# Feed-forward products with the high and low halves of the activations side by side

## The chip, the cores and the metric

One core of a Trainium2 chip runs the whole kernel. The metric is the device time of one execution in microseconds (us); lower is better. The engines are TensorE (PE, with its weight loads shown apart as PEld), VectorE (DVE), ScalarE (ACT), GpSimd (POOL) and SyncE (SP), which issues the transfers.

## The reference

The kernel computes two layers of a hybrid encoder on 256 tokens of width 1024, in float32. What matters here are the feed-forward steps, two in each layer, so four in all:

```
def swiglu_ffn(x, g, wi, wo):
    gate, up = jnp.split(rmsnorm(x, g) @ wi, 2, axis=-1)
    return (jax.nn.silu(gate) * up) @ wo
...
for l in range(DEPTH):                                          # 2
    x = x + 0.5 * swiglu_ffn(x, ffn1_norm[l], ffn1_wi[l], ffn1_wo[l])   # wi 1024 x 5632, wo 2816 x 1024
    h = rmsnorm(x, mix_norm[l])
    ...                                                         # four mixers, merged, through w_out, added to x
    x = x + 0.5 * swiglu_ffn(x, ffn2_norm[l], ffn2_wi[l], ffn2_wo[l])
```

## The kernel before

Activations are held transposed: channels on the 128 partitions, the T = 256 tokens along the columns, so x is KT = 8 tiles of 128x256. A weight tile is 128x128 and is the stationary operand; the activations move past it.

Every float32 operand is split into a high part, rounded to the type float32r, and a low part, what is left. A product is then three matmuls, which mm (L205) issues: high weights by high activations (L207), high weights by low activations (L208), low weights by high activations (L209). All three add into the same 128x256 of PSUM.

Weights come by DMA in chunks of up to 2048 columns and are split on the chip by Weights.split in units of 1024 columns, which are eight tiles: ScalarE writes hi (L109), VectorE writes lo (L110). There are four buffers of each, and W.next splits two units ahead of the one in use. The helper split (L211) does the same for activations: ScalarE at L214 (L217 with a scale), VectorE at L215 (L218).

Norm holds what a feed-forward step or the mixer takes as input: add(k) splits x times the gain, without the normalising factor; square sums squares; scale (L341) sums over partitions on TensorE (tile pr), and GpSimd takes the power -1/2 (rt); scale_rows (L353) spreads it over the partitions with four matmuls into pb (L357) and ScalarE copies it to rr (L365). So the feed-forward products start before the factor is known, and it is multiplied in behind them.

ffn (L381) runs over 11 pairs c of columns of the hidden layer. For each c, gates(c) makes two groups of eight weight tiles by three matmuls into one PSUM bank (pg), ups(c) the same into another (pu). scaled (L392) multiplies each by rr on VectorE (L395), silu applies Silu on ScalarE (L403), hidden multiplies both (L407) and splits the result into hh and hl. For c = 0 the factor is not there yet; its silu and hidden come in c = 1, behind scale_rows. Then come eight groups over 22 weight tiles into po, each added to x by VectorE (L434), after which nxt(n) prepares the norm of the next stage, or writes the output.

The mixer makes a normalised copy of x of its own for its later products: full_norm(k) takes x times gain times rr on VectorE (xnt, L511) and splits it (xnh, xnl).

PSUM has eight buffers of one bank (128x512 float32). The pool m4 has 16 buffers of 128x1040, small has two for each name. The order of instructions on each engine is made by the framework's list scheduler from the order of the program; each engine then works its list in order.

Of the kernel before, what the change touches and what calls it, by code (L numbers as in the profile page):

```python
# [9 lines left out]
F32R = mybir.dt.float32r  # L10
AF = mybir.ActivationFunctionType
ALU = mybir.AluOpType
# [5 lines left out]
T = 256  # L18
P = 128
KT = D // P  # L20
DFF = 2816
KF = DFF // P
# [20 lines left out]
O_N1, O_NM, O_N2 = 0, 8, 16  # L43
# [129 lines left out]
def hybrid_encoder(ctx: ExitStack, tc: tile.TileContext, xT, par, rows, ident_d, flat, out, order=None):  # L173
    nc = tc.nc
    A, V, G, TE = nc.scalar, nc.vector, nc.gpsimd, nc.tensor
# [9 lines left out]
    W = Weights(nc, flat, order, raw_pool, hi_pool, lo_pool)  # L185

    def bank(name):
        return ps.tile([P, 512], F32, tag="ps", name=name)

    def m4(name, dt=F32, cols=1024):  # L190
        assert cols <= 1040
        return mp.tile([P, 1040], dt, tag="m4", name=name, bufs=16)[:, :cols]
# [9 lines left out]
    def small(name, shape, bufs=2):  # L202
        return sp.tile(shape, F32, tag="s_" + name, name=name, bufs=bufs)

    def mm(out, lhs, rhs, start, stop):  # L205

        TE.matmul(out, lhs[0], rhs[0], start=start, stop=False)  # L207
        TE.matmul(out, lhs[0], rhs[1], start=False, stop=False)  # L208
        TE.matmul(out, lhs[1], rhs[0], start=False, stop=stop)  # L209

    def split(hi, lo, src, scale=None):  # L211

        if scale is None:
            a = A.copy(hi, src)  # L214
            b = V.tensor_tensor(lo, src, hi.bitcast(F32), op=ALU.subtract)  # L215
        else:
            a = A.activation(hi, src, AF.Copy, scale=scale)  # L217
            b = V.scalar_tensor_tensor(lo, src, scale, hi.bitcast(F32), op0=ALU.mult, op1=ALU.subtract)  # L218
        return a, b
# [9 lines left out]
    gains, x = xg[:, :KT], xg[:, KT:].rearrange("p (k t) -> p k t", t=T)  # L229
# [11 lines left out]
    def col(l, o, n=1):  # L241
        if l == 0 and o + n <= KT:
            return gains[:, o : o + n]
        return prm[:, l * NPAR + o : l * NPAR + o + n]
# [73 lines left out]
    class Norm:  # L318


        def __init__(self, l, gcol):
            self.l, self.gcol, self.first = l, gcol, l == 0 and gcol == O_N1
            self.hi = [m4("xh", F32R).rearrange("p (k t) -> p k t", t=T) for _ in range(2)]
            self.lo = [m4("xl", F32R).rearrange("p (k t) -> p k t", t=T) for _ in range(2)]
            self.acc, self.squared = small("acc", [P, T]), 0
            self.pairs = [(self.hi[k // 4][:, k % 4, :], self.lo[k // 4][:, k % 4, :]) for k in range(KT)]

        def add(self, k):
            return split(*self.pairs[k], x[:, k, :], scale=col(self.l, self.gcol + k))
# [23 lines left out]
        def scale_rows(self):  # L353

            pb = bank("pb")
            for b in range(2):
                TE.matmul(  # L357
                    pb[:, b * P : (b + 1) * P],
                    self.rt[:, b : b + 1].to_broadcast([P, P]),
                    ident,  # L360
                    start=True,
                    stop=True,
                )
            self.rr = small("rr", [P, T])
            A.copy(self.rr, pb[:, :T])  # L365

    def group(dst, name, l, kts, c0, pairs):

        for i, k in enumerate(kts):
            mm(dst, W.next(name, l, k, c0, P), pairs[i], i == 0, i == len(kts) - 1)  # L370

    def groups(dsts, name, l, kts, c0s, pairs, late):

        cut = len(kts) - late
        for part in (range(cut), range(cut, len(kts))):
            for dst, c0 in zip(dsts, c0s):
                for i in part:
                    mm(dst, W.next(name, l, kts[i], c0, P), pairs[i], i == 0, i == len(kts) - 1)


    def ffn(l, wi, wo, nrm, nxt):  # L381
        hs, ts, hh = [], {}, []

        def gates(c, done=0):
            for j in range(done, 2):
                group(ts["g", c][:, j * T : (j + 1) * T], wi, l, range(KT), (2 * c + j) * P, nrm.pairs)

        def ups(c, done=0):
            for j in range(done, 2):
                group(ts["u", c][:, j * T : (j + 1) * T], wi, l, range(KT), DFF + (2 * c + j) * P, nrm.pairs)  # L390

        def scaled(name, c):  # L392
            t = t2k(name)
            rr2 = nrm.rr.unsqueeze(1).to_broadcast([P, 2, T])
            V.tensor_tensor(  # L395
                t.rearrange("p (j t) -> p j t", t=T), ts.pop((name, c)).rearrange("p (j t) -> p j t", t=T), rr2, op=ALU.mult
            )
            return t

        def silu(c):  # L400
            t = scaled("g", c)
            s = ts["s", c] = t2k("s")
            A.activation(s, t, AF.Silu)  # L403

        def hidden(c):
            u = scaled("u", c)
            V.tensor_tensor(u, u, ts.pop(("s", c)), op=ALU.mult)  # L407
            if c % 2 == 0:
                hh.append((m4("hh", F32R), m4("hl", F32R)))
            o = (c % 2) * 512  # L410
            split(*(h[:, o : o + 512] for h in hh[-1]), u)
            for j in range(2):
                hs.append(tuple(h[:, o + j * T : o + (j + 1) * T] for h in hh[-1]))

        for c in range(KF // 2):
            ts["g", c], ts["u", c] = bank("pg"), bank("pu")
            if c == 0:
                groups((ts["g", 0][:, 0:T], ts["u", 0][:, 0:T]), wi, l, range(KT), (0, DFF), nrm.pairs, 2)
                gates(0, 1)
                nrm.scale()  # L420
                ups(0, 1)
                continue
            gates(c)
            if c == 1:
                nrm.scale_rows()
                silu(0)
                hidden(0)
            silu(c)
            ups(c)
            hidden(c)  # L430
        for n in range(KT):
            po = bank("po")[:, :T]
            group(po, wo, l, range(KF), n * P, hs)
            V.scalar_tensor_tensor(x[:, n, :], po, 0.5, x[:, n, :], op0=ALU.mult, op1=ALU.add)  # L434
            nxt(n)


# [36 lines left out]
    def mixer(l, nrm, tabs, nxt):  # L474
# [26 lines left out]
        evac(pl0, lat, 0, hl, True)  # L501
        evac(pl1, lat, hl, hl, True)


        xnh = [m4("xnh", F32R).rearrange("p (k t) -> p k t", t=T) for _ in range(2)]
        xnl = [m4("xnl", F32R).rearrange("p (k t) -> p k t", t=T) for _ in range(2)]
        xn = [(xnh[k // 4][:, k % 4, :], xnl[k // 4][:, k % 4, :]) for k in range(KT)]

        def full_norm(k):
            t = small("xnt", [P, T])  # L510
            V.scalar_tensor_tensor(t, x[:, k, :], col(l, O_NM + k), nrm.rr, op0=ALU.mult, op1=ALU.mult)  # L511
            split(*xn[k], t)

        qkv = [m3("qkv", cols=N_QKV) for _ in range(2)]
        pq0 = tok_group(C_QKV, hq, "w_in", nrm.pairs, range(KT))
        for k in range(4):
            full_norm(k)
        evac(pq0, qkv, 0, hq, True)
        pq1 = tok_group(C_QKV + hq, hq, "w_in", nrm.pairs, range(KT))
        for k in range(4, KT):  # L520
            full_norm(k)
        evac(pq1, qkv, hq, hq, True)


# [614 lines left out]
```

## Time and profile before

| | us |
|---|---|
| median of three runs (1385.9 to 1386.23) | 1386.22 |
| the profiled execution | 1386.98 |
| its span, first to last instruction | 1385.2 |
| TensorE busy in the span | 1367.8 |
| VectorE busy | 939.7 |
| ScalarE busy | 798.0 |

A group of instructions in a profile row has its line in the kernel, its engine, its operation, the tile written and those read by the program's names, and its shapes; L207 is line 207. The time of one matmul in such a row runs from its start to the end of its result, and matmuls overlap, so the step from one start to the next is shorter than that. Durations are of one profiled execution.

### The profile page before, as it was taken

The numbers are of one execution on the slowest core, as the hardware profiler recorded it, in microseconds if no ns is written. First come the engines' busy times: TensorE is split into PE (matmuls) and PEld (weight loads), VectorE is DVE, ScalarE is ACT, GpSimd is POOL, SyncE is SP. The second block draws the span as 40 slices with busy tenths as digits, with TensorE's granted clock in tenths as the row PEclk, the third lists the DMA queues.
The fourth block names the chain that finished last, engine by engine and source line by source line (L and its number), as shares of the span: only waits on it lengthen the run. The fifth ranks groups of instructions, "written<-read, shape, count | busy, mean of one in ns | idle before, by whom it ended". The sixth has DMA issues, their size and how long they took to land. (4 is left out here: it accounts for less than half of the span.)

```text
span 1385.2 us, 26443 instructions
## 1 busy us (share of the span) xinstructions
PE 1367.8 (99%) x11184; PEld 1356.3 (98%) x11184; DVE 939.7 (68%) x1302; ACT 798.0 (58%) x1224; POOL 90.6 (7%) x126
## 2 busy tenths in 40 slices
PE   8999999999999999999999999999999999999999
PEld 7999999999999999999999999999999999999999
DVE  6666557968966766666566665588698666776653
ACT  6444448788657655444444444487885674554442
POOL 3200002300400000000000000030013000000000
PEclk9999999999999999999999999999999999999999
DMA  7555545434543455555555555455345443555552
GB/s 286 183 183 183 185 173 192 169 128 140 190 177 134 143 185 182 184 189 189 185 181 187 189 186 183 151 183 183 119 151 194 164 153 122 201 181 183 186 204 74
DMA packets 35831, 240.81 MB, mean 174 GB/s; under 512 B 3968, under 2 KB 5376, under 8 KB 9472
## 3 DMA queue, kind: packets, MB, share of 16 engines
q1 hardware_dynamic: 35712, 239.12, 49.0%
q8 instruction: 87, 1.43, 0.4%
q14 instruction: 32, 0.26, 0.1%
HBM read 238.06 MB, written 1.05 MB: 173 GB/s over the span
## 5 line engine op out<-in xcount | busy, mean ns | idle before, releaser
L109 ACT CAST hi<-raw 128x1024 fp32r<-128x1024 f32 (+4 forms) x459 | 475.7, 1037 | 496.1 <-PE po L208 117.8
L110 DVE TENSOR_TENSOR lo<-raw,hi 128x1024 fp32r<-128x1024 f32 (+4 forms) x459 | 553.3, 1208 | 294.4 <-ACT hi L109 293.5
L207 PE MATMUL pg<-xh,hi 128*128 128x256 f32 x704 | 199.0, 283 | 5.8 <-ACT hi L109 5.8
L208 PE MATMUL pg<-xl,hi 128*128 128x256 f32 x704 | 199.5, 283 | 0.0
L209 PE MATMUL pg<-xh,lo 128*128 128x256 f32 x704 | 199.3, 283 | 0.0
L209 PE MATMUL pu<-xh,lo 128*128 128x256 f32 x704 | 198.3, 282 | 0.5 <-DVE lo L110 0.5
L208 PE MATMUL pu<-xl,hi 128*128 128x256 f32 x704 | 198.6, 282 | 0.0
L207 PE MATMUL pu<-xh,hi 128*128 128x256 f32 x704 | 198.5, 282 | 0.0
L208 PE MATMUL po<-hl,hi 128*128 128x256 f32 x704 | 197.9, 281 | 0.0
L209 PE MATMUL po<-hh,lo 128*128 128x256 f32 x704 | 197.4, 280 | 0.0
L207 PE MATMUL po<-hh,hi 128*128 128x256 f32 x704 | 197.3, 280 | 0.0
L207 PE MATMUL pgt<-xnh,hi 128*128 128x256 f32 x512 | 145.7, 285 | 0.0
L208 PE MATMUL pgt<-xnl,hi 128*128 128x256 f32 x512 | 144.6, 282 | 0.0
L209 PE MATMUL pgt<-xnh,lo 128*128 128x256 f32 x512 | 144.0, 281 | 0.0
L207 PEld LDWEIGHTS pg<-xh,hi 128*128 128x128 f32 x704 | 133.7, 190 | 6.1 <-ACT hi L109 6.1
L209 PEld LDWEIGHTS pg<-xh,lo 128*128 128x128 f32 x704 | 133.8, 190 | 0.3 <-DVE lo L110 0.2
L208 PEld LDWEIGHTS pg<-xl,hi 128*128 128x128 f32 x704 | 133.8, 190 | 0.0
L209 PEld LDWEIGHTS pu<-xh,lo 128*128 128x128 f32 x704 | 133.1, 189 | 0.7 <-DVE lo L110 0.7
L208 PEld LDWEIGHTS pu<-xl,hi 128*128 128x128 f32 x704 | 133.1, 189 | 0.0
L207 PEld LDWEIGHTS pu<-xh,hi 128*128 128x128 f32 x704 | 133.0, 189 | 0.0
L207 PEld LDWEIGHTS po<-hh,hi 128*128 128x128 f32 x704 | 132.6, 188 | 0.0
L209 PEld LDWEIGHTS po<-hh,lo 128*128 128x128 f32 x704 | 132.5, 188 | 0.0
(298 smaller groups left out, 2869.3 us busy)
## 6 DMA issues: line engine op xcount, KB each, us to landing
raw<-weights SPq DMA_DIRECT2D x205, 1024.0 KB, 4.8
raw<-weights SPq DMA_DIRECT2D x9, 768.0 KB, 4.3
raw<-weights SPq DMA_DIRECT2D x4, 896.0 KB, 4.6
raw<-weights SPq DMA_DIRECT2D x3, 1008.0 KB, 4.7
raw<-weights SPq DMA_DIRECT2D x5, 512.0 KB, 8.2
out<-xg SPq DMA_DIRECT2D x8, 128.0 KB, 2.5
raw<-weights SPq DMA_DIRECT2D x1, 1016.0 KB, 4.7
raw<-weights SPq DMA_DIRECT2D x1, 968.0 KB, 4.7
```

Source lines behind the costliest of these rows:

```text
L109: a = self.nc.scalar.copy(hi[:, :w], src)
L110: b = self.nc.vector.tensor_tensor(lo[:, :w], src, hi[:, :w].bitcast(F32), op=ALU.subtract)
L207: TE.matmul(out, lhs[0], rhs[0], start=start, stop=False)
L208: TE.matmul(out, lhs[0], rhs[1], start=False, stop=False)
L209: TE.matmul(out, lhs[1], rhs[0], start=False, stop=stop)
```

## The change

In the feed-forward products the high and low parts of an activation tile stand side by side in one tile of 512 columns. mm2 issues two matmuls for a weight tile: high weights by both halves into a whole PSUM bank (512 columns), then low weights by the high half into its first 256 columns. The two halves of a bank are added afterwards: joined copies the second half on ScalarE and adds the first on VectorE; for po, two accumulations into x do it. Each of the four groups of a c has a bank of its own. For c = 0 and 1 the products take x times the gain as before, and joined multiplies by rr; from c = 2 on they take a normalised copy of x, which normalised makes in c = 1, behind scale_rows. scale_rows comes after the first of the two gate groups of c = 1, no longer after both. The mixer's full_norm is replaced by the same function.

```diff
--- before.py
+++ after.py
@@ -208,6 +208,23 @@
         TE.matmul(out, lhs[0], rhs[1], start=False, stop=False)
         TE.matmul(out, lhs[1], rhs[0], start=False, stop=stop)
 
+    def mm2(out, lhs, both, start, stop):
+
+
+        TE.matmul(out, lhs[0], both, start=start, stop=False)
+        TE.matmul(out[:, :T], lhs[1], both[:, :T], start=False, stop=stop)
+
+    def pair_tiles(name, n):
+
+        ts = [m4(name, F32R) for _ in range((n + 1) // 2)]
+        boths = [ts[k // 2][:, k % 2 * 512 : k % 2 * 512 + 512] for k in range(n)]
+        return ts, boths, [(a[:, :T], a[:, T:]) for a in boths]
+
+    def parts(t):
+
+        t3 = t.rearrange("p (k w t) -> p k w t", k=2, t=T)
+        return t3[:, :, 0, :], t3[:, :, 1, :]
+
     def split(hi, lo, src, scale=None):
 
         if scale is None:
@@ -320,10 +337,8 @@
 
         def __init__(self, l, gcol):
             self.l, self.gcol, self.first = l, gcol, l == 0 and gcol == O_N1
-            self.hi = [m4("xh", F32R).rearrange("p (k t) -> p k t", t=T) for _ in range(2)]
-            self.lo = [m4("xl", F32R).rearrange("p (k t) -> p k t", t=T) for _ in range(2)]
+            _, self.boths, self.pairs = pair_tiles("xh", KT)
             self.acc, self.squared = small("acc", [P, T]), 0
-            self.pairs = [(self.hi[k // 4][:, k % 4, :], self.lo[k // 4][:, k % 4, :]) for k in range(KT)]
 
         def add(self, k):
             return split(*self.pairs[k], x[:, k, :], scale=col(self.l, self.gcol + k))
@@ -363,11 +378,25 @@
                 )
             self.rr = small("rr", [P, T])
             A.copy(self.rr, pb[:, :T])
+            self.full = None
+
+        def normalised(self, k):
+
+            if self.full is None:
+                self.full = pair_tiles("xn", KT)
+            t = small("xnt", [P, T])
+            V.scalar_tensor_tensor(t, x[:, k, :], col(self.l, self.gcol + k), self.rr, op0=ALU.mult, op1=ALU.mult)
+            split(*self.full[2][k], t)
 
     def group(dst, name, l, kts, c0, pairs):
 
         for i, k in enumerate(kts):
             mm(dst, W.next(name, l, k, c0, P), pairs[i], i == 0, i == len(kts) - 1)
+
+    def wide(dst, name, l, kts, c0, boths):
+
+        for i, k in enumerate(kts):
+            mm2(dst, W.next(name, l, k, c0, P), boths[i], i == 0, i == len(kts) - 1)
 
     def groups(dsts, name, l, kts, c0s, pairs, late):
 
@@ -379,59 +408,74 @@
 
 
     def ffn(l, wi, wo, nrm, nxt):
-        hs, ts, hh = [], {}, []
-
-        def gates(c, done=0):
-            for j in range(done, 2):
-                group(ts["g", c][:, j * T : (j + 1) * T], wi, l, range(KT), (2 * c + j) * P, nrm.pairs)
-
-        def ups(c, done=0):
-            for j in range(done, 2):
-                group(ts["u", c][:, j * T : (j + 1) * T], wi, l, range(KT), DFF + (2 * c + j) * P, nrm.pairs)
-
-        def scaled(name, c):
+        hs, ts = [], {}
+        NEAR = 2
+
+        def tile_of(c, j, name):
+            ts[name, c, j] = bank("p" + name)
+            return ts[name, c, j]
+
+        def column(name, c, j):
+            return (DFF if name == "u" else 0) + (2 * c + j) * P
+
+        def products(name, c, js=(0, 1)):
+            boths = nrm.boths if c < NEAR else nrm.full[1]
+            for j in js:
+                wide(tile_of(c, j, name), wi, l, range(KT), column(name, c, j), boths)
+
+        def joined(name, c):
+
             t = t2k(name)
-            rr2 = nrm.rr.unsqueeze(1).to_broadcast([P, 2, T])
-            V.tensor_tensor(
-                t.rearrange("p (j t) -> p j t", t=T), ts.pop((name, c)).rearrange("p (j t) -> p j t", t=T), rr2, op=ALU.mult
-            )
+            for j in range(2):
+                p, tj = ts.pop((name, c, j)), t[:, j * T : (j + 1) * T]
+                A.copy(tj, p[:, T:])
+                V.tensor_tensor(tj, p[:, :T], tj, op=ALU.add)
+            if c < NEAR:
+                t3 = t.rearrange("p (j t) -> p j t", t=T)
+                V.tensor_tensor(t3, t3, nrm.rr.unsqueeze(1).to_broadcast([P, 2, T]), op=ALU.mult)
             return t
 
         def silu(c):
-            t = scaled("g", c)
+            t = joined("g", c)
             s = ts["s", c] = t2k("s")
             A.activation(s, t, AF.Silu)
 
         def hidden(c):
-            u = scaled("u", c)
+            u = joined("u", c)
             V.tensor_tensor(u, u, ts.pop(("s", c)), op=ALU.mult)
-            if c % 2 == 0:
-                hh.append((m4("hh", F32R), m4("hl", F32R)))
-            o = (c % 2) * 512
-            split(*(h[:, o : o + 512] for h in hh[-1]), u)
-            for j in range(2):
-                hs.append(tuple(h[:, o + j * T : o + (j + 1) * T] for h in hh[-1]))
+            tiles, boths, _ = pair_tiles("hh", 2)
+            split(*parts(tiles[0]), u.rearrange("p (j t) -> p j t", t=T))
+            hs.extend(boths)
 
         for c in range(KF // 2):
-            ts["g", c], ts["u", c] = bank("pg"), bank("pu")
             if c == 0:
-                groups((ts["g", 0][:, 0:T], ts["u", 0][:, 0:T]), wi, l, range(KT), (0, DFF), nrm.pairs, 2)
-                gates(0, 1)
+                firsts = tile_of(0, 0, "g"), tile_of(0, 0, "u")
+                for part in (range(KT - 2), range(KT - 2, KT)):
+                    for dst, c0 in zip(firsts, (0, DFF)):
+                        for k in part:
+                            mm2(dst, W.next(wi, l, k, c0, P), nrm.boths[k], k == 0, k == KT - 1)
+                products("g", 0, (1,))
                 nrm.scale()
-                ups(0, 1)
+                products("u", 0, (1,))
                 continue
-            gates(c)
             if c == 1:
+                products("g", 1, (0,))
                 nrm.scale_rows()
                 silu(0)
                 hidden(0)
+                products("g", 1, (1,))
+                for k in range(KT):
+                    nrm.normalised(k)
+            else:
+                products("g", c)
             silu(c)
-            ups(c)
+            products("u", c)
             hidden(c)
         for n in range(KT):
-            po = bank("po")[:, :T]
-            group(po, wo, l, range(KF), n * P, hs)
-            V.scalar_tensor_tensor(x[:, n, :], po, 0.5, x[:, n, :], op0=ALU.mult, op1=ALU.add)
+            po = bank("po")
+            wide(po, wo, l, range(KF), n * P, hs)
+            for h in range(2):
+                V.scalar_tensor_tensor(x[:, n, :], po[:, h * T : (h + 1) * T], 0.5, x[:, n, :], op0=ALU.mult, op1=ALU.add)
             nxt(n)
 
 
@@ -501,24 +545,15 @@
         evac(pl0, lat, 0, hl, True)
         evac(pl1, lat, hl, hl, True)
 
-
-        xnh = [m4("xnh", F32R).rearrange("p (k t) -> p k t", t=T) for _ in range(2)]
-        xnl = [m4("xnl", F32R).rearrange("p (k t) -> p k t", t=T) for _ in range(2)]
-        xn = [(xnh[k // 4][:, k % 4, :], xnl[k // 4][:, k % 4, :]) for k in range(KT)]
-
-        def full_norm(k):
-            t = small("xnt", [P, T])
-            V.scalar_tensor_tensor(t, x[:, k, :], col(l, O_NM + k), nrm.rr, op0=ALU.mult, op1=ALU.mult)
-            split(*xn[k], t)
-
         qkv = [m3("qkv", cols=N_QKV) for _ in range(2)]
         pq0 = tok_group(C_QKV, hq, "w_in", nrm.pairs, range(KT))
         for k in range(4):
-            full_norm(k)
+            nrm.normalised(k)
+        xn = nrm.full[2]
         evac(pq0, qkv, 0, hq, True)
         pq1 = tok_group(C_QKV + hq, hq, "w_in", nrm.pairs, range(KT))
         for k in range(4, KT):
-            full_norm(k)
+            nrm.normalised(k)
         evac(pq1, qkv, hq, hq, True)
 
 
```

## Rows read from the trace of the kernel before

**Rows 1.** The page, busy time of each engine, share of the span, instructions.

```profile
PE 1367.8 (99%) x11184; PEld 1356.3 (98%) x11184; DVE 939.7 (68%) x1302; ACT 798.0 (58%) x1224; POOL 90.6 (7%) x126
```

**Rows 2.** Groups by line and form: count | busy us, mean ns of one | idle before, releasers.

```profile
L110 DVE TENSOR_TENSOR lo<-raw,hi 128x1024 fp32r<-128x1024 f32 x422 | 516.8, 1227 | 269.8 <-ACT hi L109 268.8
...
L207 PE MATMUL pg<-xh,hi 128*128 128x256 f32 x704 | 199.0, 283 | 5.8 <-ACT hi L109 5.8
...
L207 PE MATMUL pu<-xh,hi 128*128 128x256 f32 x704 | 198.5, 282 | 0.0
...
L207 PE MATMUL po<-hh,hi 128*128 128x256 f32 x704 | 197.3, 280 | 0.0
...
L395 DVE TENSOR_TENSOR g<-pg,rr 128x512 f32<-128x512 f32 x44 | 30.3, 689 | 14.6 <-PE pg L209 14.5
...
L434 DVE SCALAR_TENSOR_TENSOR xg<-po,xg 128x256 f32<-128x256 f32 x32 | 13.5, 422 | 23.9 <-PE po L209 23.9
...
L961 ACT COPY o<-pov 64x256 f32<-64x256 f32 x32 | 11.8, 368 | 6.0 <-PE pov L959 5.3
...
L511 DVE SCALAR_TENSOR_TENSOR xnt<-xg,prm,rr 128x256 f32<-128x256 f32 x16 | 7.1, 482 | 0.4 <-ACT rr L365 0.4
...
L1013 DVE TENSOR_TENSOR xg<-pw,xg 128x256 f32<-128x256 f32 x16 | 6.8, 422 | 5.1 <-PE pw L209 4.9
```

**Rows 3.** Stretches: c = 2 to 10, then po, of both feed-forward steps of layer 0.

```profile
core 0: us, PE busy (x) PEld busy (x) DVE busy (x) ACT busy (x) POOL busy (x), PEclk, DMA share, GB/s
33.15:136.11 102.96, 102.96 (x866) 102.96 (x865) 66.00 (x77) 48.25 (x55) 10.30 (x32) 1.00 0.54 183
136.11:198.64 62.53, 62.53 (x530) 62.53 (x529) 36.04 (x45) 28.70 (x38) 0.00 (x0) 1.00 0.51 179
...
530.50:632.74 102.24, 102.24 (x866) 102.24 (x865) 67.71 (x73) 48.22 (x54) 0.00 (x0) 1.00 0.53 186
632.74:695.34 62.60, 62.60 (x531) 62.60 (x530) 36.16 (x45) 28.90 (x37) 0.00 (x0) 1.00 0.53 185
```

**Rows 4.** Timeline of PE: first matmuls of ups and of the next ups, 96 steps apart.

```profile
61.75 0.28 PE L207 MATMUL pu<-xh,hi 128*128 128x256 f32 x1
...
73.19 0.28 PE L207 MATMUL pu<-xh,hi 128*128 128x256 f32 x1
```

**Rows 5.** Waits: who waited for whom, us in total, times, longest.

```profile
ACT hi L109 <- PE po L208: 117.8, 72, 2.1
ACT hi L109 <- PE pu L208: 108.9, 73, 2.3
```

**Rows 6.** Timeline of PE in the mixer: 512-column matmuls, twelve from the first row to the last.

```profile
346.42 0.39 PE L207 MATMUL pa<-hi,kvh 128*128 128x512 f32 x1
...
346.88 0.40 PE L209 MATMUL pa<-hi,kvl 128*128 128x512 f32 x1
347.12 0.39 PE L207 MATMUL pa<-hi,kvh 128*128 128x512 f32 x1
347.34 0.39 PE L208 MATMUL pa<-lo,kvh 128*128 128x512 f32 x1
...
349.19 0.27 PE L468 MATMUL pT<-ident,pe 128*128 128x128 f32 x1
```

**Rows 7.** Timeline of PE, second feed-forward step: gates of c = 1, pb, gates of c = 2.

```profile
518.69 0.28 PE L207 MATMUL pg<-xh,hi 128*128 128x256 f32 x1
...
524.37 0.60 PE L357 MATMUL pb<-ident,rt 128*128 128x128 f32 x4
...
530.50 0.28 PE L207 MATMUL pg<-xh,hi 128*128 128x256 f32 x1
```

**Rows 8.** Timeline of ACT in the same place: start us, us.

```profile
525.41 0.36 ACT L365 COPY rr<-pb 128x256 f32<-128x256 f32 x1
```

**Rows 9.** Timeline of DVE right behind it.

```profile
526.68 0.68 DVE L395 TENSOR_TENSOR g<-pg,rr 128x512 f32<-128x512 f32 x1
527.28 0.68 DVE L395 TENSOR_TENSOR u<-pu,rr 128x512 f32<-128x512 f32 x1
```

**Rows 10.** A stretch of the first mixer that holds its normalised copy of x.

```profile
214.25:232.00 17.75, 17.75 (x106) 17.75 (x105) 15.27 (x31) 15.77 (x38) 3.79 (x13) 1.00 0.63 215
```

## Prediction

> **What bounds the kernel now.** I read the page's busy times first, then the groups by line and form, then the stretches of a feed-forward stage, then single steps of TensorE in the timeline. The reader should see in [rows 1] that TensorE is busy for 99% of the span, so that only time on its own queue counts, unless a change leaves it without operands. In [rows 2] the feed-forward products (outputs pg, pu, po) are nine groups of 704 matmuls, of which three are shown: 704 x 3 = 2112 weight tiles, each passed over three times with 256 columns, and hardly any idle time stands before them. The groups' durations of about 282 ns are no prices, since matmuls overlap; the price is the step from one start to the next. [rows 3] gives it by stage: columns of c = 2 to 10 take 102.96 and 102.24 us for 9 x 32 = 288 tiles, 357.5 and 355.0 ns a tile, and the products into po 62.53 and 62.60 us for 176 tiles, 355.3 and 355.7. I take 356 ns a tile, 118.7 ns a matmul; the single stretch in [rows 4] (96 steps from 61.75 to 73.19 us) gives 119.2. In all of these stretches the granted clock is 1.00 and TensorE is never idle. VectorE and ScalarE are busy for 64% and 47% of the first stretch of [rows 3], and the waits in [rows 5] say that the cast of weights waits for TensorE to give a buffer back: weights are ready ahead of time. So 2112 x 0.356 = 752 us of the time are steps of these matmuls and nothing else.
>
> **The matmuls.** Columns per tile stay 768: 3 x 256 before, 512 + 256 after. What goes is one matmul and one weight load of three. If a step is strictly in proportion to columns, nothing is gained. The trace of before has 512-column matmuls in the mixer, with the same 128x128 weight load before each: twelve steps from 346.42 to 349.19 us in [rows 6] are 2.77 us, 231 ns each. Twice 118.7 is 237, so a part of about 6 ns of each step does not grow with its columns. The pair would take 231 + 119 = 349.5 ns against 356: 6.5 ns x 2112 = **-13.7 us**. This is the value I take, because shape, type and load are those of the new matmul. Single steps in [rows 6] go from 220 ns (347.12 to 347.34) to 240 (346.88 to 347.12), with 10 ns of rounding in each; as ends for a mean I take 224 and 236. At 236 a tile saves 1.3 ns, 3 us in all; at 224 it saves 13 ns, 28 us. The trace does not show 512 and 256 columns in turn; I see no reason in it for a different price of the mixed order.
>
> The Trainium skill (TensorE: Matmul & The Clock Gate, Back-to-back issue gap) gives a warm step as columns / 2.4 GHz plus about 2.5 ns; by it the pair would save just that one 2.5 ns, an estimate of 5.3 us, and the sum below would end about 8 us higher. The rows do not agree with it in size: by it 256 columns would take 109 ns, and they take 119.
>
> **Joining the two halves.** Each group of eight tiles now fills a bank of its own (high half and low half of the activations), and per column pair c there are four ScalarE copies of 128x256 from PSUM and four VectorE additions of 128x256. In [rows 2] the nearest rows are the copy of po's kind in the mixer (o<-pov, 368 ns, 64 partitions) and xg<-pw,xg, 422 ns. For c of 2 or more the two scalings by rr (689 ns each) go. VectorE: +4 x 0.42 - 2 x 0.69 = +0.3 us per c; ScalarE: +4 x 0.37 = +1.5 us per c. A c takes TensorE 11.2 us, VectorE now uses 66.00 / 9 = 7.3 and ScalarE 48.25 / 9 = 5.4 of it [rows 3]; 7.6 and 6.9 after. Both lie beside TensorE: nothing. The cover is the weights held ahead; without it the four copies would cost 1.5 us a c. A c holds four of the eight banks; a bank is wanted again after eight groups of 2.8 us and is given back about a microsecond after its group ends: nothing, unless a join is queued behind something late. After the last c, the hidden tile's chain (two copies, two additions, one product, one split, about 3 us) has 20 tiles x 0.35 = 7 us before po wants it: nothing.
>
> **The normalised copy of x.** From c = 2 on, the products take x already normalised: per FFN eight times one VectorE product (482 ns, xnt), one ScalarE cast and one VectorE subtraction (nearest: 422 ns). They can't begin before rr, and c = 2 can't begin without their first result. This is the one new wait, and what queues behind it is TensorE itself. In the second FFN [rows 7] the sums of pb start at 524.37 us after both pg groups of c = 1; rr is written by ScalarE at 525.41 + 0.36, [rows 8]; c = 2 starts at 530.50. The change calls scale_rows after one of the two pg groups, half of 524.37 - 518.69 earlier, so rr comes at about 522.9 and c = 2 wants tile 0 some 7.6 us later and tile 7 after 7 x 0.35 = 2.5 us more: a cover of 10.1 us. In it VectorE has: two scalings, one product and one split for c = 0 (4 x 0.69 = 2.8), the eight pairs (8 x 0.90 = 7.2), and one or two splits of weights at 1.23: 11.2 to 12.4 us. Instructions that follow at once overlap a little (starts at 526.68 and 527.28 for durations of 0.68 [rows 9]), 0.08 x 22 = 1.8 us less: 9.4 to 10.6. The additions for c = 0 do not need rr, and lie in VectorE's idle time before it. So the chain is about as long as its cover. If all of it fits, nothing; if every step waits for the one before (0.48 + 0.37 + 0.42 = 1.3 us by eight, 2.8 for c = 0, two splits and a 512-column silu and cast or so) it is about 17 us, 7 too long. I take 1.25 us a FFN, near the lower end because the two engines work on different k at once: **+5 us** for four, bounds 0 and 28. The weights lag a little behind after it, which three units of 2.8 us held ahead hide.
>
> **The small ones.** The two accumulations into x instead of one (xg<-po,xg, 422 ns, [rows 2]) lie beside 7.7 us of matmuls in each po group, but the last stands at the end: **+0.4 us**. At the start the first matmul waits for the low part of x too, at most one operation like xnt's 482 ns, inside a start that waits for weights: 0. In the mixer only names move; the order that the scheduler makes may shift by something: 0.
>
> **The sum.** The profiled execution took 1386.98 us (span 1385.2). 1386.98 - 13.7 + 5 + 0.4 = 1378.7; the median of the runs is 0.76 lower, so 1377.9: I say **1378**.
>
> **Rivals.** *Steps in proportion to columns.* For it: most of a step is columns; against it: 231 is not 237. With 3 us saved and 0 to 5.4 us paid, 1383 to 1389: no change. The fixed piece of the Trainium skill (TensorE: Matmul & The Clock Gate, Back-to-back issue gap), by estimate 5.3 us saved, would come out in the same stretch. *The normalised copy as a new bound, which ends slower.* Place: the start of c = 2 in each FFN. It decides from 13.3 / 4 = 3.3 us of idle TensorE per FFN, where the gain is gone, and from 4.0 us it is slower by over 0.2%. With 6 us, 24 in all: 1386.2 - 13.3 + 24 = 1397. For it: 10 us of VectorE work in a cover of 10 us, ScalarE's table load and casts between; against it: the mixer does the same eight steps today beside other work, 15.27 us of VectorE and 15.77 of ScalarE in a stretch of 17.75 in which TensorE is never idle [rows 10]. *A larger piece per step.* If 512 columns take 224 ns here, or hiding one load less helps, 28 us are saved: 1364 with 5.4 paid. For it: the lower steps of [rows 6]; against it: their mean.
>
> **How the numbers follow.** Forecast, 1372 to 1383: 0.46. Proportional, or a gain just given back, 1383 to 1389: 0.18. New bound, 1389 to 1404: 0.22. Larger piece, 1359 to 1372: 0.14. The range 1366 to 1392 leaves out about 0.06 below and 0.14 above. A difference under 0.2% (2.8 us) can't be told from none here. Faster 0.60, same 0.18, slower 0.22, from the same cases; the forecast alone gives 1372 to 1383.
>
> **What would show it.** After: steps of 512 columns at 231 ns and of 256 at 119 in pg, pu and po (a tile every 349.5 ns, 100.7 us for nine c, 61.5 for po); idle time of PE before the first pg of c = 2 under 2 us, with xnl or xnh as releaser if there is any; VectorE some 65 us busier (per FFN 9 x 0.3 and 2 x 1.7 in the joins, 7.2 for the copies, 3.4 in po) and ScalarE some 78 (44 x 0.37 and 8 x 0.4), with no idle TensorE from them elsewhere. Wrong: a tile at 355 ns or more, PE waiting for hi or lo in the middle of c = 2 to 4, PE waiting for a bank, or a mixer that is longer by microseconds.

## The result, and the profile after

| | us |
|---|---|
| before, median of 4 | 1386.06 |
| changed, median of 4 (1398.64 to 1400.16) | 1399.6 |
| ratio of the two, 95% interval | 1.0098 (1.0085 to 1.011) |
| the profiled execution of the changed kernel, its span | 1399.43, 1397.6 |

The changed kernel is 1% slower. The range ended at 1392; the rival that ends slower, the normalised copy as a new bound, gave 1397.

The page of the changed kernel, busy times; it answers to [rows 1]:

```profile
PE 1363.8 (98%) x9072; PEld 1256.2 (90%) x9072; DVE 990.1 (71%) x1502; ACT 852.3 (61%) x1432; POOL 90.7 (6%) x126
```

TensorE is busy for 4 us less in a span that is 12.4 us longer: about 16 us more in which it does nothing. The waits say where:

```profile
PE pg L214 <- DVE xn L232: 13.2, 5, 3.6
...
PE pr L362 <- DVE acc L352: 2.3, 1, 2.3
```

Five waits for xn, the normalised copy, 13.2 us in all, and one of 2.3 us at the start for the sum of squares. Neither wait is among those of before.

Next, stretches of the changed kernel in the second feed-forward step: the end of c = 1, the wait, and what follows it; then c = 4 to 10 and po, which answer to [rows 3].

```profile
core 0: us, PE busy (x) PEld busy (x) DVE busy (x) ACT busy (x) POOL busy (x), PEclk, DMA share, GB/s
528.12:533.72 5.60, 5.60 (x34) 4.79 (x32) 5.44 (x11) 4.26 (x9) 0.00 (x0) 1.00 0.51 187
533.72:537.48 3.76, 0.17 (x2) 0.00 (x1) 3.46 (x7) 2.44 (x5) 0.00 (x0) 1.00 0.59 187
537.48:541.94 4.46, 4.46 (x16) 3.84 (x17) 4.38 (x11) 1.60 (x4) 0.00 (x0) 0.62 0.18 77
...
561.92:640.51 78.59, 78.59 (x450) 68.90 (x449) 52.94 (x71) 44.21 (x70) 0.00 (x0) 1.00 0.55 188
640.51:702.20 61.69, 61.69 (x355) 54.11 (x353) 38.64 (x52) 28.96 (x38) 0.00 (x0) 1.00 0.55 188
```

In steady work the change does what it was said to do: 78.59 us for seven c of 32 tiles is 350.8 ns a tile, and 61.69 us for 176 tiles 350.5, against 355 to 357.5 in [rows 3]. What is lost is lost around the start of c = 2. TensorE waits from 533.9 to 537.48, and in the stretch behind it the granted clock is 0.62 in the mean. The timeline of PE shows the wait and the two levels:

```profile
533.61 0.28 PE L215 MATMUL pu<-xh,lo 128*128 128x256 f32 x1
537.48 0.51 PE L214 MATMUL pg<-xn,hi 128*128 128x512 f32 x1 [3.59 <-DVE xn L232]
...
538.92 0.63 PE L214 MATMUL pu<-xn,hi 128*128 128x512 f32 x1
539.34 0.41 PE L215 MATMUL pu<-xn,lo 128*128 128x256 f32 x1
539.56 0.63 PE L214 MATMUL pg<-xn,hi 128*128 128x512 f32 x1
```

A tile takes 0.64 us there (538.92 to 539.56) in place of 0.35: the clock has gone from 2.4 to 1.2 GHz after 3.6 us of idleness. The 16 matmuls from 537.48 to 541.94 take 4.46 us where eight tiles need 2.80, so the wait costs another 1.7 us. The other three steps show the same at the same place: waits of 1.8 and 0.9 us in the first, 3.6 us in the third and 3.3 us in the fourth. With them the granted clock is at 0.50 for 3.4 us in the first and the third step and for 6.8 us in the fourth.

What VectorE did from rr to the first finished tile of the copy, in order:

```profile
526.02 1.23 DVE L110 TENSOR_TENSOR lo<-raw,hi 128x1024 fp32r<-128x1024 f32 x1 [1.58 <-ACT hi L109]
527.17 0.69 DVE L435 TENSOR_TENSOR g<-g,rr 128x512 f32<-128x512 f32 x1
527.77 0.88 DVE L388 SCALAR_TENSOR_TENSOR xnt<-xg,prm,rr 128x256 f32<-128x256 f32 x2
528.81 0.76 DVE L432 TENSOR_TENSOR u<-pu,u 128x256 f32<-128x256 f32 x2 [0.16 <-ACT u L431]
529.48 0.74 DVE L432 TENSOR_TENSOR g<-pg,g 128x256 f32<-128x256 f32 x2
530.14 0.68 DVE L435 TENSOR_TENSOR u<-u,rr 128x512 f32<-128x512 f32 x1
530.74 0.69 DVE L435 TENSOR_TENSOR g<-g,rr 128x512 f32<-128x512 f32 x1
531.34 1.22 DVE L110 TENSOR_TENSOR lo<-raw,hi 128x1024 fp32r<-128x1024 f32 x1
532.48 0.69 DVE L445 TENSOR_TENSOR u<-u,s 128x512 f32<-128x512 f32 x1
533.08 1.22 DVE L110 TENSOR_TENSOR lo<-raw,hi 128x1024 fp32r<-128x1024 f32 x1
534.21 0.42 DVE L432 TENSOR_TENSOR u<-pu,u 128x256 f32<-128x256 f32 x1
534.93 1.23 DVE L110 TENSOR_TENSOR lo<-raw,hi 128x1024 fp32r<-128x1024 f32 x1 [0.30 <-ACT hi L109]
536.07 0.42 DVE L432 TENSOR_TENSOR u<-pu,u 128x256 f32<-128x256 f32 x1
536.41 0.68 DVE L232 TENSOR_TENSOR hh<-u,hh 128x512 fp32r<-128x512 f32 x1
537.01 0.76 DVE L232 TENSOR_TENSOR xn<-xnt,xn 128x256 fp32r<-128x256 f32 x2
```

and ScalarE's part in it:

```profile
533.85 1.04 ACT L109 CAST hi<-raw 128x1024 fp32r<-128x1024 f32 x1 [0.96 <-ACT u L431]
534.81 0.36 ACT L431 COPY u<-pu 128x256 f32<-128x256 f32 x1
535.07 0.62 ACT L231 CAST hh<-u 128x512 fp32r<-128x512 f32 x1
535.59 0.71 ACT L231 CAST xn<-xnt 128x256 fp32r<-128x256 f32 x2
538.79 0.80 ACT L231 CAST xn<-xnt 128x256 fp32r<-128x256 f32 x2 [2.50 <-DVE xnt L388]
```

VectorE stands still for half a microsecond in 11. The copy's first two products come early, at 527.77, but their casts stand in ScalarE's list behind a cast of weights, the copy of u's last half (534.81) and hh. That copy of u reads the last pu group of c = 1, which TensorE ends at 533.89 (533.61 + 0.28). So the list puts the casts of xn behind work that begins only when TensorE has run out of it, and the first tile is ready 9 us after its product. The third and the fourth step have the same order; in the first the casts come ahead of the copies of u, and the wait is the shortest of the four. From 526.02 to the first tile VectorE does four splits of weights, six additions, three scalings, and the product and the subtraction of the hidden tile of c = 0.

### The profile page after: what moved, and what is told of

The parts are those of the page before. It is cut to its first block, busy times and chain, and to the rows that moved or that the text cites. A ratio compares the mean times of both kernels' runs of the same rounds, so it can differ in the third digit from the quotient of the medians.

```text
span 1397.6 us, 22651 instructions
## 1 busy us (share of the span) xinstructions
PE 1363.8 (98%) x9072; PEld 1256.2 (90%) x9072; DVE 990.1 (71%) x1502; ACT 852.3 (61%) x1432; POOL 90.7 (6%) x126
## 5 line engine op out<-in xcount | busy, mean ns | idle before, releaser
L214 PE MATMUL po<-hh,hi 128*128 128x512 f32 x704 | 246.5, 394 | 0.0
L214 PE MATMUL pg<-xn,hi 128*128 128x512 f32 x576 | 208.6, 401 | 13.3 <-DVE xn L232 13.2
L214 PE MATMUL pu<-xn,hi 128*128 128x512 f32 x576 | 207.8, 399 | 0.0
L215 PE MATMUL pg<-xn,lo 128*128 128x256 f32 x576 | 163.5, 284 | 0.0
L215 PE MATMUL pu<-xn,lo 128*128 128x256 f32 x576 | 162.2, 283 | 0.0
L207 PE MATMUL pgt<-xn,hi 128*128 128x256 f32 x512 | 145.2, 284 | 0.0
L208 PE MATMUL pgt<-xn,hi 128*128 128x256 f32 x512 | 143.8, 281 | 0.0
L209 PE MATMUL pgt<-xn,lo 128*128 128x256 f32 x512 | 143.3, 280 | 0.0
L215 PEld LDWEIGHTS pg<-xn,lo 128*128 128x128 f32 x576 | 110.5, 192 | 0.6
L215 PEld LDWEIGHTS pu<-xn,lo 128*128 128x128 f32 x576 | 110.1, 191 | 0.5
L207 PEld LDWEIGHTS pgt<-xn,hi 128*128 128x128 f32 x512 | 96.3, 188 | 1.0
L208 PEld LDWEIGHTS pgt<-xn,hi 128*128 128x128 f32 x512 | 96.4, 188 | 0.1
```

The costliest lines, as they stand in the source:

```text
L214: TE.matmul(out, lhs[0], both, start=start, stop=False)
L215: TE.matmul(out[:, :T], lhs[1], both[:, :T], start=False, stop=stop)
```

## The experiments

**Theories.** A: the copy is late at c = 2, by its place in the lists, and TensorE's idle time and the clock behind it eat the gain. B: the joins load ScalarE and VectorE too much everywhere. Four runs first, with before at 1385.87 us.

*Without the copy* (e1). joined multiplies by rr for every c.

```diff
-        NEAR = 2
+        NEAR = KF // 2
...
-                for k in range(KT):
-                    nrm.normalised(k)
```

> The wide products without the normalised copy of x: every c takes x times the gain, and joined multiplies by rr for all c, as the kernel before does. Theory A (the copy of x is late; TensorE idles for 2.7 to 3.6 us before c = 2 of each of the four feed-forward steps, 13.2 us in all, and then runs some 3.4 us at half the clock each time): these two go, some 13 + 7 us, about 1380 us, faster than before by 0.3 to 0.6%. Theory B (the joins, 176 more ScalarE copies and 88 more VectorE additions than products saved, load the two engines too much everywhere): still 1392 us or more, with TensorE waiting in the middle of c = 2 to 10.

Measured 1372.63 us, ratio 0.9904 (0.989 to 0.9919): 27.0 us less than the changed kernel, and faster than before by more than theory A asked for. From c = 1 on TensorE waits for no activation in its feed-forward steps. c = 2 to 10 and po of the same step:

```profile
526.30:626.87 100.57, 100.57 (x579) 88.38 (x578) 80.73 (x111) 58.30 (x91) 0.00 (x0) 1.00 0.56 189
626.87:688.57 61.70, 61.70 (x355) 53.91 (x354) 39.17 (x53) 28.95 (x38) 0.00 (x0) 1.00 0.56 188
```

VectorE is busy for 80% of the first stretch, more than in the changed kernel, and TensorE for all of it. Theory B falls.

*Eight buffers for xnt* (e2). The eight products of the copy go to m4 tiles of their own.

```diff
...
-            t = small("xnt", [P, T])
+            if own and k % 4 == 0:
+                self.xnt = m4("xnt")
+            t = self.xnt[:, k % 4 * T : k % 4 * T + T] if own else small("xnt", [P, T])
...
```

> The changed kernel with eight buffers for xnt in the feed-forward steps in place of two. Theory A1 (the copy is late because only two of eight tiles can be under way, four rounds of product, cast and subtraction at 1.7 to 2.1 us each): the idle time before c = 2 falls below 1 us, about 1385 us. Theory A2 (it is late because its first casts stand behind other work in ScalarE's list, 8 us after the first products): the first cast comes no earlier, at most half of the idle time goes, 1391 to 1399 us.

Measured 1407.16 us, ratio 1.0155 (1.0138 to 1.0172), slower still: the waits at c = 2 are 10.3, 4.8, 4.8 and 4.9 us. In the second step the first products now stand at 540.15 in VectorE's list, behind the same joins and splits, and the casts right behind them:

```profile
540.15 1.66 DVE L390 SCALAR_TENSOR_TENSOR xnt<-xg,prm,rr 128x256 f32<-128x256 f32 x4
```

A1 falls: more buffers do not bring it forward, and in the changed kernel the products of the first two tiles were done by 528.7, so two buffers were not what made the first tile late. Neither expected time was met; the list came out in another order, and why the scheduler put the products later with more room stays open.

*The copy first used for c = 4* (e3).

```diff
-        NEAR = 2
+        NEAR = 4
```

> The changed kernel, but the normalised copy is first used for c = 4 in place of c = 2; it is still made in c = 1. Theory A (a matter of when the copy is wanted): 22 us more cover, no idle time before c = 2 or c = 4, about 1380 us. Rival (VectorE and ScalarE can't do the copy and the joins and the weights in this part at all): the idle time moves to c = 4 or to waits for weights, 1392 us or more.

Measured 1373.43 us, ratio 0.9911 (0.9897 to 0.9926). No wait for xn is left. The copy is still spread over all the time there is; its last subtraction is at 547.54, and c = 4 starts at 549.21:

```profile
547.54 0.41 DVE L232 TENSOR_TENSOR xn<-xnt,xn 128x256 fp32r<-128x256 f32 x1
```

So the work fits; the moment at which it is wanted decides. And the copy buys nothing: e1, which scales for every c, is no slower than this run.

*Narrow matmuls in the changed kernel* (e4).

```diff
-        TE.matmul(out, lhs[0], both, start=start, stop=False)
+        TE.matmul(out[:, :T], lhs[0], both[:, :T], start=start, stop=False)
+        TE.matmul(out[:, T:], lhs[0], both[:, T:], start=False, stop=False)
```

> The changed kernel with each matmul of 512 columns cut into two of 256 over the same operands and the same two halves of the bank: three matmuls and three weight loads a tile, all else as changed. If a 512-column step is 231 ns against 2 x 118.5, this costs 6 ns x 2112 = 13 us more than the changed kernel, about 1412 us, less what the four stalls shrink because c = 1 takes longer. If steps go by columns alone, no change: 1399 us.

Measured 1403.0 us, ratio 1.0123 (1.0108 to 1.0138): 3.4 us more than the changed kernel, not 13. The waits at c = 2 are shorter by half (1.9 us in place of 3.6), so this run can't tell the price of a step. The next one can.

**The price of a step, and the order.** Four more runs, before at 1385.58 us.

*Narrow matmuls without the copy* (e4b): the edits of e1 and e4 together.

> The kernel without the normalised copy (every c multiplied by rr), with each matmul of 512 columns cut into two of 256: three matmuls and three weight loads a tile, nothing else different from that kernel, which took 1372.6 us and has no idle time at c = 2 that would hide or shift anything. If 512 columns cost 231 ns against 2 x 118.5, this is 6 to 6.5 ns x 2112 = 13 to 14 us slower, about 1386 us. If the gain came from elsewhere (the layout, the joins, the weight buffers given back earlier), it stays near 1373.

Measured 1377.58 us, ratio 0.9948 (0.9933 to 0.9963): 5.0 us slower than with wide matmuls, and 8 us faster than before with the same three matmuls a tile. Neither theory had this. The 5.0 us are not spread evenly: the gates and ups of the first step take 5.5 us more than in e1 (its profile has 3.4 us there at a granted clock of 0.50), those of the last step 2.2 us less. Its steps, taken from start to start without those that wait, sum to 352.1 ns a tile in the mean of all stages, where before has 355.9 and the wide kernel 350.1: 3.8 x 2112 = 8.0 us and 2.0 x 2112 = 4.2 us. What makes the 3.8 ns is asked below.

*The sum of squares one group later* (e5), with the edit of e1.

```diff
                 products("g", 0, (1,))
-                nrm.scale()
                 products("u", 0, (1,))
+                nrm.scale()
```

> The kernel without the normalised copy, and the sum over partitions (pr) behind both second groups of c = 0 in place of behind the first. In the run without this the sum of the first step waits 1.9 us for the last square. If nothing else moves, that wait goes: about 1370.7 us. If rr then comes too late for the joins of c = 0 (it has one group less), banks are held and it is not faster than 1372.6.

Measured 1369.6 us, ratio 0.9892 (0.9876 to 0.9909), the fastest of all: 1.1% below before, 2.1% below the changed kernel. The wait for acc is gone, and TensorE waits for nothing that hangs on rr. In the profiles 2.3 us of the gain over e1 lie in the first step; 1.5 lie in the second mixer, where e1 has 3.4 us at a granted clock of 0.50 and this run has none, so they are not the sum's.

*The copy ahead of silu and hidden* (e6).

```diff
                 nrm.scale_rows()
+                for k in range(KT):
+                    nrm.normalised(k)
                 silu(0)
                 hidden(0)
                 products("g", 1, (1,))
-                for k in range(KT):
-                    nrm.normalised(k)
```

> The changed kernel with the eight steps of the normalised copy written right behind scale_rows, ahead of silu and hidden of c = 0. Theory C (the copy is late because of its place: between rr and the need of c = 2 VectorE's list holds some 11 us of joins, scalings and weight splits ahead of the first finished tile, and VectorE is busy for 17.8 of 18.5 us there): the first tile is ready some 7 us earlier, the idle time before c = 2 falls under 1 us, about 1376 to 1382 us. Theory D (the two engines have too much work in these 18 us, in whatever order): the idle time moves to a wait for weights or for a bank, 1390 us or more.

Measured 1386.7 us, ratio 1.001 (1.0001 to 1.0019). Place alone gives 12.9 of the 27.0 us back: the waits for xn fall from 13.2 to 1.5 us. The waits of e6 (us in all, how many, the longest) show what is left for xn:

```profile
PE pg L214 <- DVE xn L232: 1.5, 2, 1.2
```

But its c = 2 to 10 of the second step take 103.30 us, not 100.57, as the windows of the same kernel show:

```profile
534.40:637.70 103.30, 102.17 (x578) 88.30 (x577) 75.13 (x107) 59.63 (x99) 0.00 (x0) 1.00 0.53 184
```

As in the changed kernel, the scheduler mixes the four groups of c = 2, a tile of the copy at a time, which holds all four weight buffers open. By the starts of the matmuls, c = 2 and c = 3 take 12.4 and 12.3 us here and each later c 11.2: 2.3 of the 2.7 us, of which 1.1 are waits that the profile shows, for weights and tiles. Of the 14.1 us that e6 is slower than e1, the gates and ups of the four steps from c = 1 on hold 10.2; 1.4 lie at the start and 3.0 in the mixers, where this copy is neither made nor used. So place is a bit more than half of what the copy costs. That the rest is the amount of work in c = 1 to 3 (theory D) is argued from e3, where a later need removes it, and not shown by itself.

*Wide products into po alone* (e7), on the kernel before: hidden tiles as pairs of halves, mm2 for po, two accumulations into x.

> The kernel before with wide matmuls for the products into po alone: hidden tiles as pairs of halves, two accumulations into x, no joins, no copy of x; gates and ups as before. With 6 to 6.5 ns a tile, 704 tiles: 4.2 to 4.6 us less, 0.4 us more at the end, about 1382 us. If the gain depends on something that only the gate products have, no change: 1386 us.

Measured 1382.49 us, ratio 0.9985 (0.9976 to 0.9994): 3.1 us less, against 3.8 to 4.2 expected net. Po takes 350.2 to 350.7 ns a tile; before it took 355.3 to 355.8 in three of the steps, and 350.0 in the last, where nothing was left to gain.

**Where the other 8 us come from.** Theory P: a step depends on where the moving operand lies. Theory Q: it is the other half of the PSUM bank. Before at 1385.97 us.

*The kernel before with the halves side by side* (e8), still three matmuls of 256 columns into the same 256.

```diff
-            self.hi = [m4("xh", F32R)... for _ in range(2)]
-            self.lo = [m4("xl", F32R)... for _ in range(2)]
+            _, self.pairs = pair_tiles("xh", KT)
...
-                hh.append((m4("hh", F32R), m4("hl", F32R)))
+            ts2, two = pair_tiles("hh", 2)
...
```

> The kernel before, three matmuls of 256 columns into the same 256 columns of PSUM, but with the high and low halves of x and of the hidden tiles side by side in one tile, as the change lays them. In the run with narrow matmuls and all else wide, a tile took 352.1 ns where the kernel before takes 355.9, over 2112 tiles 8 of its 8 us. Theory P (where the moving operands lie sets part of a step; in the trace of before the same tile and part take the same step to within 1 ns in all eight groups of po, and different tiles from 112 to 129): a tile at another figure, 350 to 354 ns, about 1378 us. Theory Q (the other half of the bank for the second matmul makes the step shorter): 355.9 ns, 1386 us.

Measured 1376.75 us, ratio 0.9933 (0.9919 to 0.9948): 9 us faster than before, without a wide matmul, a join or a copy. Its tiles take 352.6 ns in the mean of all stages, so 7.0 of the 9.2 us are in these products.

*Narrow, without the copy, high and low parts apart* (e10): e4b with hi and lo in tiles of their own.

> The kernel without the normalised copy and with narrow matmuls (1377.6 us), but with high and low parts in tiles of their own as in the kernel before; the products of the high weights still go to the two halves of the bank. Theory Q: as with the halves side by side, 352 ns and 1378 us. Theory P: back toward the kernel before, 354 to 357 ns, 1382 to 1388 us.

Measured 1389.79 us, ratio 1.0023 (1.0012 to 1.0035), a little above the range of theory P; its tiles take 355.9 ns, as before, and its start has a wait of 1.9 us for the sum of squares. The windows of c = 2 to 10 in the last step of four kernels follow. With the parts apart, the kernel before:

```profile
1217.08:1320.27 103.19, 103.19 (x866) 103.19 (x865) 66.64 (x73) 47.34 (x54) 0.00 (x0) 1.00 0.53 185
```

Apart too, e10:

```profile
1219.40:1322.59 103.19, 103.19 (x866) 103.19 (x865) 80.13 (x111) 60.37 (x92) 0.00 (x0) 1.00 0.52 186
```

Side by side, e4b:

```profile
1210.26:1309.62 99.36, 99.36 (x866) 99.36 (x865) 80.19 (x111) 60.50 (x92) 0.00 (x0) 1.00 0.54 193
```

Side by side, e8:

```profile
1209.56:1308.92 99.36, 99.36 (x867) 99.36 (x865) 66.66 (x73) 47.31 (x54) 0.00 (x0) 1.00 0.55 192
```

The pairs agree to 0.01 us although two of the kernels use one half of the bank and two both, and although two have VectorE 13 us busier. Theory Q falls; the layout of the moving operands decides: 288 tiles at 358.3 ns apart, 345.0 side by side. The wide kernel e1 takes 101.31 us in this stage, more than the narrow ones side by side:

```profile
1203.88:1305.19 101.31, 101.31 (x578) 88.44 (x577) 80.79 (x113) 61.09 (x93) 0.00 (x0) 1.00 0.55 188
```

*The kernel before with m4 padded* (e9), and the fastest version padded (e11): `mp.tile([P, 1040]` becomes `mp.tile([P, 1056]`.

> The kernel before with tiles of the pool m4 padded from 1040 to 1056 columns, nothing else: the same instructions with the activations at other addresses. Theory P: the mean tile of some stages moves by 2 ns or more from 355.9 and the time by 2 to 10 us, either way. Theory Q: 355.9 ns and 1386 us.

Measured 1388.14 us, ratio 1.0015 (1.0005 to 1.0024). The stages move, as theory P has it (gates of the last step from 357.9 to 353.4 ns a tile, its po from 350.0 to 355.8), but against each other, and the time by only 2 us.

> The fastest version so far (no normalised copy, late sum, wide matmuls, 1369.6 us) with m4 padded to 1056. If wide steps depend on place as narrow ones do, its tile moves from 350.1 ns by 2 ns or more and the time by 4 us or more; if they hardly do, 350 ns and 1368 to 1371 us.

Measured 1377.4 us, ratio 0.9941 (0.9926 to 0.9956). The wide tile stays at 350.8 ns, but the time rises by 7.8 us all the same: from the start of the first mixer to the second step, and of the second to the last, 308.6 and 309.6 us where e5 had 306.1 and 305.0. The mixers' matmuls, narrow ones, use tiles of the same pool. But place is not all of it: in the profile of e11 each mixer has 3.4 us at a granted clock of 0.50, which costs 1.7 us each, and that of e5 has none. So wide steps hardly depend on place, and padding takes back half of the 16 us that the fastest version is ahead of before; how much of that is addresses and how much the clock in the mixers is not shown.

## Why the prediction was wrong

**The normalised copy of x** is the step that failed: "I take 1.25 us a FFN ... +5 us for four, bounds 0 and 28". The mechanism was named and its place was right; the term was mis-sized. The changed kernel is 27.0 us slower than e1, and the starts of the stages divide that: 22.7 us from c = 1 on in the gates and ups of the four steps, 5.7 a step in place of 1.25, with 7 as the upper bound; 2.9 at the start of the kernel, and 1.4 in the mixers. The second step's gates and ups, changed and without the copy:

```profile
510.38:640.51 130.13, 126.42 (x714) 110.32 (x713) 90.47 (x132) 73.49 (x120) 1.61 (x1) 0.99 0.51 178
...
502.99:626.87 123.88, 123.88 (x715) 108.89 (x714) 95.75 (x134) 71.81 (x112) 1.60 (x1) 1.00 0.55 188
```

Three things in the working of this term were wrong.
- "The additions for c = 0 do not need rr, and lie in VectorE's idle time before it": those of g do, those of u stand behind rr, at 528.81, and the joins of c = 1, which the sum left out, come before the copy too. With four splits instead of one or two, VectorE had 11 us of work ahead of the first finished tile, where I counted all eight tiles of the copy into 10.6.
- A sum of work is not a place in a list. The first casts stood on ScalarE behind the copy of the last group of c = 1, which ends when TensorE has nothing left. e6 shows what the place is worth: 12.9 us.
- The clock was left out. In the second and the third step a wait of 3.6 us is followed by 3.4 us at 1.2 GHz, 1.7 us more; in the fourth, 6.8 us at 1.2 GHz cost 3.0. The trace of before had a case to read it from, in the first mixer, where TensorE waits 1.3 us for a low part of weights and the granted clock of the stretch is 0.87 in the mean:

```profile
480.00:493.00 13.00, 11.54 (x81) 11.04 (x81) 8.13 (x16) 4.61 (x9) 0.00 (x0) 0.87 0.41 156
```

**The matmuls**, -13.7: the size was nearly right, the reason was not, so the fit is in part luck. A tile went from 355.9 to 350.1 ns, 12.2 us, with 231.7 and 118.5 ns for the two steps where 231 and 118.7 were taken. But e8 gets 7.0 us in these products with narrow matmuls, so more than half of what I read as a fixed piece of each step was the place of the operands in the kernel before. What is left for width is the 5.0 us between e4b and e1, 4.2 of them in the steps, and that is a mean over places: by stage, a tile of e4b takes from 6.5 ns more to 6.3 ns less than one of e1. The Trainium skill (TensorE: Matmul & The Clock Gate, Back-to-back issue gap) has a fixed 2.5 ns in the gap of an isolated matmul, by estimate 5.3 us for one matmul less a tile: the two runs agree with it in total, though not stage by stage, and the larger saving of the prediction does not. The gap that the Trainium skill gives by this for 256 columns, about 109 ns, stays below every stage mean here, 115.0 to 119.8 ns.

**The joins**, nothing: right. e1 has all of them and TensorE never waits for one; VectorE is 80% busy there. Their size was not: in the changed kernel VectorE is busy for 50 us more than before and ScalarE for 54, where 65 and 78 were forecast.

**The mixers**, 0: they are 3.4 us shorter than before in the profiles. It is not only names that move there: the mixers' operands got the new layout too.

**The start**, 0: wrong by some 5 us. The first matmul starts 0.8 us later than before. The sum of squares waited 2.3 us behind a split and a join, and the next 5.26 us, for eight tiles, ran at a clock of 0.50:

```profile
17.24:20.70 3.46, 1.16 (x7) 0.88 (x5) 3.46 (x6) 1.38 (x3) 0.00 (x0) 0.82 1.00 417
20.70:25.96 5.26, 5.26 (x17) 4.48 (x18) 1.40 (x11) 1.04 (x1) 3.35 (x2) 0.50 0.35 125
```

Part of this is in the 27.0 us: in e1 the same wait is 1.9 us and the clock stays at 1.00 behind it, so 0.4 us of the wait and all of the clock's 2.5 us are gone there. e5 takes the wait away.

**The rivals.** The new bound came true, and by a cost that it did not count: the waits for xn are 3.3 us a step, where by its own sum the gain is just gone; with the slow clock behind them it is 5.3, past the 4.0 from which "it is slower". "Steps in proportion to columns" and "a larger piece per step" did not come true for the wide steps, which stayed within 349 to 352 ns a tile in every stage of every run.

The 27.0 us, as far as the traces carry it: 13.2 of waits for xn; about 8 of slow clock with them (1.7 in each of the first three steps, 3.0 in the fourth); 2.9 at the start; 1.4 in the mixers. The last 1.4 or so I did not place.

## What to carry to other kernels

Before a product is made to depend on a new preparation, write down the whole list of the engine that makes it, between the moment its input is there and the moment its output is wanted, other jobs' shares included; a sum that just fits will not fit. Look above all for work in that list which itself waits for the end of what is to be covered. On TensorE add what the clock costs behind a wait, from a stretch in which the trace shows it. And when two layouts differ along with a change, run the layout alone: here it held more than half of what the wide matmuls seemed to give, at no cost.

## What the runs showed of the hardware that was not expected

The step of a 256-column float32r matmul is not one figure. In the first po stage of the kernel before, the same tile and part of a product take the same step to within 1 ns in the last six of the eight groups, while different tiles take from 112 to 128 ns. The weights of a tile lie in other places of their buffers from group to group, so these make no difference there. The first two groups do not fit: in their first 13 tiles 19 of the 39 steps are off from the other six by up to 11 ns, so the place of the moving operand is not all of it (the expectation of e8 says "all eight groups"). Stage means go from 345.0 to 359.5 ns for three such steps, and follow the layout and padding of the moving operands (e8, e9, e10). What in the address does it is open; no run here varied one address alone. Pairs of 512 and 256 columns vary far less, 349 to 352 ns a tile.
